# Norm factors spread over the partitions by way of DRAM, and the end of a convolution module written in a new order

## The chip, the cores and the metric

The kernel runs on one core of one Trainium2 chip. The metric is the device time of one execution in microseconds (us), and the smaller the better. A core has five engines that run side by side, each with its own list of instructions: TensorE (PE; its weight loads are shown as PEld), VectorE (DVE), ScalarE (ACT), GpSimd (POOL) and SyncE (SP). SP issues most of the DMAs, POOL those that add onto what stands in SBUF. An instruction starts when the one ahead of it on its engine is out of the way and the semaphores it waits for have been set.

## The reference

Four residual layers on 512 tokens of 1024 channels, all in float32: a mixer (retention and pooling), an FFN, a conformer convolution module, a second FFN. Every sub-layer reads its input through an RMS norm, and a last norm ends it. The parts that the change touches:

```python
def rms_norm(x, g):
    x32 = x.astype(jnp.float32)
    y = x32 * lax.rsqrt(jnp.mean(x32 * x32, axis=-1, keepdims=True) + EPS)
    return (y * g).astype(x.dtype)

def conformer_conv(h, w_pw1, b_pw1, w_dw, b_dw, ln_g, ln_b, w_pw2, b_pw2):
    a, gate = jnp.split(h @ w_pw1 + b_pw1, 2, axis=-1)
    u = a * jax.nn.sigmoid(gate)
    dw = lax.conv_general_dilated(
        u, w_dw[:, None, :], window_strides=(1,), padding=((CONV_WIDTH - 1, 0),),
        dimension_numbers=('NWC', 'WIO', 'NWC'), feature_group_count=D_MODEL) + b_dw
    d32 = dw.astype(jnp.float32)
    mu = jnp.mean(d32, axis=-1, keepdims=True)
    var = jnp.mean(jnp.square(d32 - mu), axis=-1, keepdims=True)
    z = (d32 - mu) * lax.rsqrt(var + EPS) * ln_g + ln_b
    z = jax.nn.silu(z).astype(h.dtype)
    return z @ w_pw2 + b_pw2

def swiglu(h, w_gate, w_up, w_down):
    return (jax.nn.silu(h @ w_gate) * (h @ w_up)) @ w_down
...
    for layer in range(DEPTH):
        ...
        h = h + swiglu(rms_norm(h, ffn_norm_g[layer]), ffn_w_gate[layer], ffn_w_up[layer], ffn_w_down[layer])
    return rms_norm(h, final_norm_g)
```

## The kernel before

**Tiling.** Activations lie with channels on the 128 partitions and the 512 tokens along the row, as eight tiles of 128 channels. Every large product is made of three: operand and weight are each split into a high part and a rest (`xgh`, `xgl`, `w`), and PE multiplies high by high, high weight by rest, rest weight by high (`mm3`, lines 199 to 201; each 128x512). `feature_major` runs over the eight k-tiles and two output tiles, 48 matmuls.

**The weights' split.** A chunk of weights (1 MB) comes by SP into `wr`. ACT copies it to the high part and writes its negative into the rest; then either DVE forms the rest (`split_load`, line 186), or a POOL DMA adds the raw chunk onto the negative (`split_load` lines 176 to 178, in the FFNs' chunk 2; `split_rest` lines 1351 to 1353, in the conv module). The latter are `w<-wr` on POOL in the profile. PE's third matmul (line 201) of a k-tile reads the rest, so it cannot start before that DMA has landed.

**The norms.** The norm's factor is one number a token. `token_sums` (line 281) sums the squares by matmuls whose weights are the 128 tokens of a block and whose moving operand is a column of ones; the result has tokens on the partitions, four columns (`ps_ms`). `rsqrt` makes the factors `rs_y` (128x4) on DVE by Newton steps. `spread` (lines 284 to 294) then brings them along the rows, the same on all partitions: four matmuls of a broadcast column with the identity into `ps_rms`, and an ACT copy to `bc_rms` (128x512). The factors are applied late, to the products: in the mixer to the rotations' cosine and sine (lines 497, 498), in the FFNs to `gu` in `hidden` (line 884), in the conv module to `gu` in `gated` (line 1191). This happens once in each of the four layers.

**The conv module.** `proj(j)` is the product for channel tile j (48 matmuls into `ps_pw`). `gated(j)` makes u: DVE scales by `bc_rms` (L1191), ACT takes the sigmoid (`act`, L1192), DVE joins them (L1196). The depthwise convolution of tiles 0 to 2 is done tap by tap on DVE (`some_taps`, L1329). For tiles 3 to 7, `to_rows` copies u by four DMAs into `R`, 32 partitions each (for tile 5 into the room of `zh`), and `conv_tile` (L1229) runs 32 matmuls of 32 columns, over 512 tokens, or over a half of 256 (A, then B) for tiles 6 and 7. `pivot_sum` takes sums of tiles 0 and 1 by PE, `pivot_tile` adds a tile to the running sums, `stats` has PE sum over the channels (L281), `spread` brings mean and scale along the rows (`mus`, `lrs`). Then `centre`, `swish`, `z_hi`, `z_lo` make the operand of the last product in pairs of tiles (`d`, `zh` L1288, `zl`), and `out_proj` runs the first two output pairs for half A, then for half B (`ps_p`, lines 220 to 223).

**What sets the order.** In the conv module the order on PE, DVE, ACT and SP is as the code is written (`manual_schedule`). In the other layers a scheduler places the instructions of each engine at build time; SP and POOL execute their lists in order as well. `split_rest` is a generator: `next(rest)` issues its first half, and `gated(..., rest)` the second half after the sigmoid. The PSUM tiles `aux` of `paux` (two) hold `ps_ms`, the spreads and the convolutions' results; `pair` gives tiles of two banks.

## Time and profile before

| what | us |
|---|---|
| median of three runs (1048.09 to 1048.49) | 1048.3 |
| the profiled execution, its own time | 1047.62 |
| its span, first instruction to last | 1045.8 |
| PE busy in the span | 1035.9 |
| DVE busy | 850.5 |
| ACT busy | 515.9 |
| POOL busy | 32.5 |

The granted TensorE clock was 0.998 over the span, so the clock plays no part. The layers on PE: the mixer to 182 us, the first FFN to 514, the conv module to 696, then the second FFN. "Idle before, releaser" behind a row is the time its engine stood still before it, and what it waited for. PE's starts lie closer together than its durations, since matmuls overlap: a 128x512 matmul takes 0.39 us in the records and the next one starts 0.23 us later.

### The profile page before, as it was taken

The numbers are of one execution on the slowest core, as the hardware profiler recorded it, in microseconds if no ns is written. First come the engines' busy times: TensorE is split into PE (matmuls) and PEld (weight loads), VectorE is DVE, ScalarE is ACT, GpSimd is POOL, SyncE is SP. The second block draws the span as 40 slices with busy tenths as digits, with TensorE's granted clock in tenths as the row PEclk, the third lists the DMA queues.
The fourth block names the chain that finished last, engine by engine and source line by source line (L and its number), as shares of the span: only waits on it lengthen the run. The fifth ranks groups of instructions, "written<-read, shape, count | busy, mean of one in ns | idle before, by whom it ended". The sixth has DMA issues, their size and how long they took to land.

```text
span 1045.8 us, 16517 instructions
## 1 busy us (share of the span) xinstructions
PE 1035.9 (99%) x6705; PEld 907.9 (87%) x6705; DVE 850.5 (81%) x1297; ACT 515.9 (49%) x881; POOL 32.5 (3%) x33
## 2 busy tenths in 40 slices
PE   9999999999999999999999999999999999999997
PEld 7878888899999999998888665988999999999987
DVE  7888735889988889997779797859999888899855
ACT  8543134765454545543444325656654455445434
POOL 0000000100000000001121100000000000000000
PEclk9999999999999999999999999999999999999999
DMA  8322122643323322333248996146233332323122
GB/s 300 132 81 81 41 81 88 184 136 116 111 92 104 119 91 92 122 118 125 81 94 188 222 189 149 59 139 174 72 121 121 102 121 76 112 96 122 41 81 81
DMA packets 38108, 121.63 MB, mean 116 GB/s; under 512 B 4112, under 2 KB 13328, under 8 KB 29584
## 3 DMA queue, kind: packets, MB, share of 16 engines
q1 hardware_dynamic: 34432, 107.99, 32.4%
q0 software_dynamic: 3456, 12.58, 6.3%
q8 instruction: 52, 0.85, 0.3%
q14 instruction: 24, 0.20, 0.1%
q10 hardware_dynamic: 144, 0.00, 0.0%
HBM read 100.36 MB, written 2.10 MB: 98 GB/s over the span
## 4 chain that ended last, share of the span: by engine, by line
PE 88%; DVE 6%; ACT 2%; DMA 2%; issue 1%; DVEq 0%; ACTq 0%
PE ps_x L854 19%; PE ps_y L854 10%; PE ps_dn L199 7%; PE ps_dn L200 7%; PE ps_dn L201 7%; PE ps_z L854 5%; PE ps_c L1229 2%; PE ps_gu L201 2%; PE ps_gu L199 2%; PE ps_gu L200 2%; PE ps_pw L199 2%; PE ps_pw L201 2%; PE ps_pw L200 2%; DMA wr<-in_w_pw 2%; PE ps_wo L201 1%; PE ps_wo L200 1%
## 5 line engine op out<-in xcount | busy, mean ns | idle before, releaser
L854 PE MATMUL ps_x<-th,w 128*128 128x256 f32 x608 | 115.9, 276 | 0.3 <-ACT sn L929 0.3
L765 DVE TENSOR_TENSOR wg<-wg 128x512 f32<-128x512 f32 x152 | 105.3, 693 | 5.1
L774 ACT CAST w<-wg 128x512 fp32r<-128x512 f32 x152 | 82.9, 618 | 37.3 <-PE ps_y L854 36.0
L854 PEld LDWEIGHTS ps_x<-th,w 128*128 128x128 f32 x608 | 97.2, 188 | 0.5 <-ACT sn L929 0.5
L779 DVE TENSOR_TENSOR w<-wg,w 128x2048 fp32r<-128x2048 f32 x38 | 87.1, 2291 | 10.5 <-ACT w L774 10.1
L854 PE MATMUL ps_x<-tl,w 128*128 128x256 f32 x304 | 83.9, 276 | 0.0
L311 DVE TENSOR_TENSOR X<-X,ps_dn 128x1024 f32<-128x1024 f32 x46 | 56.0, 1218 | 18.6 <-PE ps_dn L201 18.6
L183 ACT CAST w<-wr 128x2048 fp32r<-128x2048 f32 (+2 forms) x22 | 34.8, 1599 | 56.6 <-PE ps_g L573 21.8
L199 PE MATMUL ps_dn<-hh,dh0d 128*128 128x512 f32 x152 | 59.4, 391 | 0.0
L200 PE MATMUL ps_dn<-hl,dh0d 128*128 128x512 f32 x152 | 59.4, 391 | 0.0
L201 PE MATMUL ps_dn<-hh,dl0d 128*128 128x512 f32 x152 | 59.2, 390 | 0.1
L854 PE MATMUL ps_y<-th,w 128*128 128x256 f32 x304 | 57.9, 276 | 0.0
L854 PE MATMUL ps_y<-xgh,w 128*128 128x256 f32 x304 | 57.9, 276 | 0.0
L854 PEld LDWEIGHTS ps_x<-tl,w 128*128 128x128 f32 x304 | 57.1, 188 | 0.0
L939 ACT COPY sn<-ps_x 128x256 f32<-128x256 f32 x38 | 14.2, 374 | 85.9 <-PE ps_x L854 85.9
L200 PE MATMUL ps_dn<-hl,dh1d 128*128 128x512 f32 x144 | 56.2, 391 | 0.0
L199 PE MATMUL ps_dn<-hh,dh1d 128*128 128x512 f32 x144 | 56.2, 391 | 0.0
L201 PE MATMUL ps_dn<-hh,dl1d 128*128 128x512 f32 x144 | 56.0, 389 | 0.0
L854 PE MATMUL ps_x<-xgh,w 128*128 128x256 f32 x288 | 55.2, 277 | 0.0
L878 DVE TENSOR_TENSOR hl<-act,hh 128x512 fp32r<-128x512 f32 x44 | 30.5, 692 | 26.3 <-ACT hh L877 26.1
L877 ACT CAST hh<-act 128x512 fp32r<-128x512 f32 x44 | 27.3, 621 | 48.0 <-DVE act L872 44.0
L199 PE MATMUL ps_pw<-xgh,w 128*128 128x512 f32 x128 | 50.3, 393 | 0.0
(346 smaller groups left out, 3098.9 us busy)
## 6 DMA issues: line engine op xcount, KB each, us to landing
wg<-in_w_gu SPq DMA_DIRECT2D x38, 1024.0 KB, 4.9
dr<-in_w_dn SPq DMA_DIRECT2D x64, 256.0 KB, 2.9
w<-wr POOLq DMA_DIRECT2D x24, 512.0 KB, 5.3
wr<-in_w_pw SPq DMA_DIRECT2D x10, 1024.0 KB, 5.1
wr<-in_w_gu SPq DMA_DIRECT2D x6, 1024.0 KB, 4.9
dr<-in_w_dn SPq DMA_DIRECT2D x32, 192.0 KB, 2.5
wr<-in_w_o SPq DMA_DIRECT2D x4, 1024.0 KB, 4.9
R<-u SPq DMA_DIRECT2D x12, 270.0 KB, 14.6
```

What stands on the lines that cost most here:

```text
L183: nc.scalar.copy(wh[:, s], raw[:, s])
L199: nc.tensor.matmul(out, lhsT=wh, rhs=xh, start=start, stop=False)
L200: nc.tensor.matmul(out, lhsT=wh, rhs=xl, start=False, stop=False)
L201: nc.tensor.matmul(out, lhsT=wl, rhs=xh, start=False, stop=stop)
L311: nc.vector.tensor_tensor(xx, xx, ps, sign)
L765: nc.vector.tensor_tensor(o, o, i, ALU.add)
L774: nc.scalar.copy(block(sums[f][0], *SUMS[i]), block(raw_g[f], *SUMS[i]))
L779: nc.vector.tensor_tensor(l, raw_g[f], h.bitcast(F32), ALU.subtract)
L854: nc.tensor.matmul(out, lhsT=u[:, k, :], rhs=v, start=first and k == 0 and n == 0, stop=k == 3 and n == 2, skip_group_check=True)
L877: nc.scalar.copy(hh[f], s)
L878: return lambda: nc.vector.tensor_tensor(hl[f], s, hh[f].bitcast(F32), ALU.subtract)
L1229: nc.tensor.matmul(ps[32 * i:32 * i + 32, :n], lhsT=dgs[j][:, i, g, :], rhs=Rs[j][:, i, 4 * g + cols.start:4 * g + cols.stop], start=g == ...
```

## The change

There are two parts.

First, the four spreads of the norms' factors (`rms`) no longer use PE and ACT. A new `spread_row` has SP write `rs_y` (128x4, 2 KB) into a row in DRAM (`row_rms`) and then read that row back with the same 512 numbers to all 128 partitions (`bc_rms`, 256 KB). For the row to be in the order of the tokens, `token_sums(by=NT)` now takes as weights every fourth token (a partition then holds four neighbouring tokens) in both FFNs and the conv module; the mixer keeps its blocks and writes the row with four-byte pieces. The spreads of the conv module's `mu` and `lrs` stay on PE.

Second, the conv module from tile 5's gate on is written anew:

- The sigmoids of `gated(5)` and `gated(6)` stand ahead of the ACT copies of the weights' split, which come after the rows' DMAs.
- `pivot_sum` comes after 18 taps instead of 14; the spread of the pivot stands before group 4 of tile 4's convolution instead of 5.
- Tile 5's convolution runs in two halves, as those of 6 and 7; the gate of tile 7 too. PE's order is c5 A, c6 A, c5 B (first half), c7 A, c5 B (second half), statistics of A, c6 B, c7 B.
- `out_proj` does the products with the high parts for all four output tiles first, then those with the rests `zl`; the spread of B's mean stands in its midst.
- The first pair of half B is scaled and activated tile by tile.

```diff
+    dr = ctx.enter_context(tc.tile_pool(name="dr", bufs=2, space=bass.MemoryType.DRAM))
...
-    def token_sums(acc, cols=FULL):
+    def token_sums(acc, cols=FULL, by=1):
...
+        if by > 1:
+            for t in range(n):
+                nc.tensor.matmul(ps[:, t:t + 1], lhsT=acc.rearrange("p (q t) -> p t q", t=n)[:, t, :], rhs=ones,
+                                 start=True, stop=True)
+            return ps[:, :n]
...
+    def spread_row(v, name, tokens="(p t) -> p t"):
+        row = dr.tile([S], F32, tag="row", name=f"row_{name}")
+        out = wk.tile([P, S], F32, tag=f"bc_{name}", name=f"bc_{name}", bufs=1)
+        nc.sync.dma_start(row.rearrange(tokens, t=NT), v)
+        nc.sync.dma_start(out, row.partition_broadcast(P))
+        return out
...
-            rb = spread(rtok, "rms")
+            rb = spread_row(rtok, "rms", "(t p) -> p t")
...
-        r = inv_rms(acc)
+        row["rb"] = spread_row(inv_rms(acc), "rms")
...
-        feature_major(ps[1], *w, xgh, xgl, between={5: lambda: row.update(rb=spread(r, "rms"))})
+        feature_major(ps[1], *w, xgh, xgl)
...
-                proj(1, {2: lambda: note("rb", spread, row["r"], "rms")})
-                rb = row["rb"]
+                rb = spread_row(row["r"], "rms")
+                proj(1)
...
-                rest = split_rest()
-                next(rest)
                 c3 = conv_tile(3, FULL)
                 some_taps(1)
-                gated(5, pss[5], FULL, two_taps, rest)
+                gated(5, pss[5], FULL, two_taps)
                 start_load()
                 to_rows(5, FULL)
+                for _ in split_rest():
+                    pass
                 bias_tile(3, c3)
-                some_taps(14)
+                some_taps(18)
...
-                some_taps(8)
-                into_sums(2)
-                c5 = conv_tile(5, FULL)
-                gated(7, pss[7], FULL)
-                to_rows(7, A)
-                start_load()
-                to_rows(7, B)
+                into_sums(2, two_taps)
+                some_taps(NDVE * CW)
+                pivot_tile(4, c4, FULL)
+                into_sums(1)
+                p5 = pair("ps_c5")
+                c5 = conv_tile(5, A, ps=p5[:, 0, :])
+                for cols in HALVES:
+                    gated(7, pss[7], cols)
+                    to_rows(7, cols)
+                    if cols is A:
+                        start_load()
...
                 c6 = conv_tile(6, A, ps=p6[:, 0, :])
-                pivot_tile(5, c5, FULL)
+                pivot_tile(5, c5, A)
+                c5 = conv_tile(5, B, ps=p5[:, 1, :], groups=range(4))
                 c7 = conv_tile(7, A, ps=p7[:, 0, :])
...
+                conv_tile(5, B, ps=p5[:, 1, :], groups=range(4, 8))
...
-                swish(0, B)
-                z_hi(0, B)
+                for i in range(2):
+                    di = d[:, i, B]
+                    nc.vector.tensor_tensor(di, di, lrs[:, B], ALU.mult)
+                    nc.scalar.activation(di, di, AF.Silu, scale=V("ln_g", i), bias=V("ln_b", i))
+                    nc.scalar.copy(zh[:, i, B], di)
```

Where the instructions stand, as the built programs have them (no time is in this). Line numbers of after.py run one or two above those of before. **PE at the end of the conv module.** Tile 5 reads its rows from `zh`, tile 6 from `R_5673` (before) or `R_5663` (after), tile 7 from `R_5834` or `R_5837`; x32 is 32 matmuls. Before:

```order
L1229 MATMUL ps_c_5794<-zh,zf_5033 32x512 x32
L1229 MATMUL ps_c_5856<-R_5673,zf_5034 32x256 x32
L1229 MATMUL ps_c_5857<-R_5834,zf_5034 32x256 x32
L1229 MATMUL ps_c_5856<-R_5673,zf_5034 32x256 x12
L281 MATMUL ps_ms<-con,acc 128x1 x2
L281 MATMUL ps_ms<-con,s_5039 128x1 x2
L1229 MATMUL ps_c_5856<-R_5673,zf_5034 32x256 x16
L289 MATMUL ps_mu<-con,mean 128x128 x2
```

And after:

```order
L1231 MATMUL ps_c_5797<-zh,zf_5029 32x256 x32
L1231 MATMUL ps_c_5854<-R_5663,zf_5030 32x256 x32
L1231 MATMUL ps_c_5797<-zh,zf_5029 32x256 x16
L1231 MATMUL ps_c_5855<-R_5837,zf_5030 32x256 x32
L1231 MATMUL ps_c_5797<-zh,zf_5029 32x256 x16
L274 MATMUL ps_ms<-con,acc 128x1 x2
L274 MATMUL ps_ms<-con,s_5035 128x1 x2
L1231 MATMUL ps_c_5854<-R_5663,zf_5030 32x256 x16
```

Half of tile 5's convolution now lies behind tile 6's first half and around tile 7's, and the twelve matmuls of c6 B that stood ahead of the statistics stand behind them.

**ACT in the conv module,** from the sigmoid of tile 4 (`act`) to that of tile 6. Before:

```order
L1192 ACTIVATE act<-gu,vec 128x512
L1351 CAST w_5444<-wr_5351 128x1024
L1352 ACTIVATE w_5444<-w_5444 128x1024
L1351 CAST w_5527<-wr_5433 128x1024
L1352 ACTIVATE w_5527<-w_5527 128x1024
L1192 ACTIVATE act<-gu,vec 128x512
L1351 CAST w_5527<-wr_5433 128x1024
L1352 ACTIVATE w_5527<-w_5527 128x1024
L1242 ACTIVATE d<-ps_c_5531,vec 128x512
```

And after:

```order
L1194 ACTIVATE act<-gu,vec 128x512
L1353 CAST w_5437<-wr_5344 128x1024
L1354 ACTIVATE w_5437<-w_5437 128x1024
L1194 ACTIVATE act<-gu,vec 128x512
L1353 CAST w_5570<-wr_5426 128x1024
L1354 ACTIVATE w_5570<-w_5570 128x1024
L1353 CAST w_5570<-wr_5426 128x1024
L1354 ACTIVATE w_5570<-w_5570 128x1024
L1244 ACTIVATE d<-ps_c_5520,vec 128x512
```

The sigmoid of tile 5 no longer stands behind the copy that waits for the chunk `wr_5433`.

**SP in the conv module.** The row and its broadcast stand between the last chunk loaded ahead and the next one. After:

```order
L148 DMA wr_5052<-in_w_pw 128x2048
L294 DMA row_rms<-rs_y 128x4
L295 DMA bc_rms<-row_rms 128x512
L148 DMA wr_5184<-in_w_pw 128x2048
L148 DMA wr_5268<-in_w_pw 128x2048
```

Before, the same chunk loads followed one another with nothing between them; in the other three layers the two DMAs are put in likewise, and POOL's list is unchanged.

**PE in the mixer.** Here the scheduler has moved some matmuls. `ps_p` with `yh` is the pooling's group map, `ps_v` a projection. The third group's rows before:

```order
L571 MATMUL ps_v_800<-w_657,xgh_107 128x512
L572 MATMUL ps_v_800<-w_657,xgh_107 128x512
L199 MATMUL ps_p_726<-yh,pwh 128x512
L573 MATMUL ps_v_800<-w_657,xgl_108 128x512
L571 MATMUL ps_v_800<-w_657,xgh_109 128x512
```

And after:

```order
L573 MATMUL ps_v_799<-w_656,xgh_109 128x512
L574 MATMUL ps_v_799<-w_656,xgh_109 128x512
L575 MATMUL ps_v_799<-w_656,xgl_110 128x512
L200 MATMUL ps_p_725<-yh,pwh 128x512
L573 MATMUL ps_v_799<-w_656,xgh_111 128x512
```

The matmul that reads `yh` stands one matmul of `ps_v` later than before; the second group's likewise, the first group's stands where it stood, the fourth's some ten rows later.

More of the change, by code (lines that the diff above doesn't have):

```diff
@@ L294, in spread @@
         return out
+    def spread_row(v, name, tokens="(p t) -> p t"):
[4 more added lines that the diff above has]
+        return out
     def inv_rms(acc):
         v = sm.tile([P, NT], F32, tag="ms", name="ms")
[L298 removed]
+        nc.vector.tensor_scalar(v, token_sums(acc, by=NT), 0.5 / D, 0.5 * EPS, ALU.mult, ALU.add)
         return rsqrt(v, NT, "a4")
@@ L1430, in conv @@
                 pivot_mean()
-                gated(6, pss[6], FULL, two_taps, rest)
+                gated(6, pss[6], FULL, two_taps)
                 to_rows(6, FULL)
-                c4 = conv_tile(4, FULL, {5: lambda: spread(row["piv"], "mu", piv)})
-                some_taps(4)
+                for _ in split_rest():
+                    pass
+                c4 = conv_tile(4, FULL, {4: lambda: spread(row["piv"], "mu", piv)})
+                some_taps(6)
                 nc.vector.scalar_tensor_tensor(s1, piv, -2.0, dsum, ALU.mult, ALU.add)
@@ L1463, in conv @@
                 centre(2, A)
-                rest = pivot_tile(6, c6, B, True)
                 swish(2, A)
@@ L1467, in conv @@
                 z_lo(0, A)
-                rest()
+                pivot_tile(6, c6, B)
                 centre(4, A)
@@ L1472, in conv @@
                 z_lo(2, A)
-                rest = pivot_tile(7, c7, B, True)
+                later = pivot_tile(7, c7, B, True)
                 centre(6, A)
-                rest()
+                later()
                 swish(6, A)
@@ L1484, in conv @@
                 note("B", stats, B)
-                out_proj(w1, 4, A)
-                spread(row["B"][0], "mu", mus[:, B])
+                out_proj(w1, 4, A, lambda: spread(row["B"][0], "mu", mus[:, B]))
                 spread(row["B"][1], "lrs", lrs[:, B])
```

48 lines of the change are left out of this document (22 added, 26 removed).

## The prediction

> **What bounds the kernel now.** I read the page's busy times and its chain first, then the waits of PE alone, then the timeline of each engine at the places that the change touches.
>
> ```profile
> PE 1035.9 (99%) x6705; PEld 907.9 (87%) x6705; DVE 850.5 (81%) x1297; ACT 515.9 (49%) x881; POOL 32.5 (3%) x33
> ...
> PE 88%; DVE 6%; ACT 2%; DMA 2%; issue 1%; DVEq 0%; ACTq 0%
> ```
>
> PE is busy for 1035.9 of the span's 1045.8 us. Little is to be had from its waits; time falls if PE has less to do, and only if what PE comes to next is ready earlier too. What the matmuls waited for, but for the first instruction of all (total, times, longest):
>
> ```profile
> PE ps_p L222 <- ACT zh L1288: 0.8, 2, 0.5
> PE ps_ms L281 <- DVE acc L1301: 0.3, 1, 0.3
> PE ps_x L854 <- ACT sn L929: 0.3, 1, 0.3
> PE ps_ms L281 <- DVE acc L256: 0.2, 1, 0.2
> ```
>
> The conv module owns the first two (1.1 us), and the change rewrites both places.
>
> **What the removed spreads cost.** Four times eight short matmuls and one ACT copy go:
>
> ```profile
> L289 PE MATMUL ps_rms<-con,rs_y x32: 271/275/275, 31.3 to 715.5; 128*128 128x128 f32 x32
> L293 ACT COPY bc_rms<-ps_rms x4: 566/568/588, 32.4 to 718.1; 128x512 f32<-128x512 f32 x4
> ```
>
> In the first FFN PE's list reads (start, duration):
>
> ```profile
> 200.47 0.39 PE L201 MATMUL ps_gu<-xgh,w 128*128 128x512 f32 x1
> 200.70 1.05 PE L289 MATMUL ps_rms<-con,rs_y 128*128 128x128 f32 x8
> 201.51 0.48 PE L199 MATMUL ps_gu<-xgh,w 128*128 128x512 f32 x1
> 201.82 0.39 PE L200 MATMUL ps_gu<-xgl,w 128*128 128x512 f32 x1
> ```
>
> Without the eight, the matmuls of 201.51 and 201.82 would start 0.23 and 0.46 after 200.47: 200.70 and 200.93. So a spread is worth 201.82 - 200.93 = 0.9 us of PE, four of them 3.6. The sum now asks, for each, what PE meets next.
>
> **Mixer: 0.2 of 0.9.**
>
> ```profile
> 40.47 0.69 DVE L497 TENSOR_TENSOR cosr<-cosr,bc_rms 128x512 f32<-128x512 f32 x1 [3.88 <-ACT cosr L494]
> ```
>
> ```profile
> 64.67 0.39 PE L200 MATMUL ps_u<-xgl,w 128*128 128x512 f32 x1
> 65.15 0.50 PE L199 MATMUL ps_p<-yh,pwh 128*128 128x512 f32 x1
> ...
> 81.06 0.39 PE L572 MATMUL ps_v<-w,xgh 128*128 128x512 f32 x1
> 81.51 0.50 PE L199 MATMUL ps_p<-yh,pwh 128*128 128x512 f32 x1
> ```
>
> The factors' first reader, DVE at 40.47, waits for ACT's cosine, not for the spread at 31, so the trip by DRAM lies in 9 us of cover. But the chain from that cosine through the rotations to `yh` runs on DVE and ACT and does not move. At 65.15 PE is already 0.25 late (0.48 after its neighbour instead of 0.23) because it waits for `yh`; coming there 0.9 sooner it waits 1.15. The spread gives nothing there. At 81.51 another 0.22 is lost to `yh`; there the new order puts one matmul of `ps_v` ahead, 0.23, which covers it. I take 0.2; bounds 0 and 0.9.
>
> **Both FFNs: 0 of 1.8.** This is where I expect the expected gain to go. The weight loads just behind the spread:
>
> ```profile
> 206.16 0.19 PEld L201 LDWEIGHTS ps_gu<-xgh,w 128*128 128x128 f32 x1 [0.26 <-DMA w<-wr]
> ```
>
> ```profile
> 720.29 0.19 PEld L201 LDWEIGHTS ps_gu<-xgh,w 128*128 128x128 f32 x1 [0.41 <-DMA w<-wr]
> ```
>
> These are the first matmuls of `ps_gu` that read the rest of chunk 2. PE already waits there for the POOL DMA that makes that rest. What sets its landing is not PE at 200:
>
> ```profile
> 199.10 1.05 ACT L176 CAST w<-wr 128x1024 fp32r<-128x1024 f32 x1 [0.26 <-DMA wr<-in_w_gu]
> 200.18 1.06 ACT L177 ACTIVATE w<-w 128x1024 fp32r<-128x1024 f32 x1
> ```
>
> ```profile
> 201.53 0.86 POOL L178 DMA_DIRECT2D w<-wr  x1 [11.78 <-ACT w L177]
> ```
>
> The chunk's load ends, ACT copies and negates, POOL issues: a chain that the change does not touch. PE gets there 0.9 sooner and waits 0.9 longer, in both FFNs. The ACT copy that goes stands behind those two and shortens nothing. The DRAM trip has cover here, from the last step of `rs_y` to its first reader:
>
> ```profile
> 197.99 0.16 DVE L271 SCALAR_TENSOR_TENSOR rs_y<-rs_t,rs_y 128x4 f32<-128x4 f32 x1
> ...
> 206.75 1.22 DVE L884 TENSOR_TENSOR gu<-ps_gu,bc_rms 128x1024 f32<-128x1024 f32 x1
> ```
>
> These are 8.6 us. Bounds for the two: +1.0 if the 256 KB of the broadcast hold up each POOL DMA by half a microsecond, -1.8 if the landing moves along. I take 0.
>
> **Conv module: the trip.** Here the factors are wanted at once:
>
> ```profile
> 532.45 0.16 DVE L271 SCALAR_TENSOR_TENSOR rs_y<-rs_t,rs_y 128x4 f32<-128x4 f32 x1
> ...
> 536.44 1.23 DVE L1191 TENSOR_TENSOR gu<-ps_pw,bc_rms 128x1024 f32<-128x1024 f32 x1 [3.79 <-ACT bc_rms L293]
> ```
>
> From `rs_y` to the gate were 3.8 us by PE and ACT. Neither new DMA is in the trace; the nearest rows, and the largest for a plain load:
>
> ```profile
> dr<-in_w_dn SPq DMA_DIRECT2D x64, 256.0 KB, 2.9
> wr<-in_w_pw SPq DMA_DIRECT2D x10, 1024.0 KB, 5.1
> dr<-in_w_dn SPq DMA_DIRECT2D x32, 192.0 KB, 2.5
> ```
>
> Two legs, one behind the other: at least 2.5 + 2.9 = 5.4, at most 2 x 5.1 = 10.2. I take 5.4, with two POOL DMAs in flight beside it: DVE starts its gates about 1.6 late, 6.4 at the upper end. Only the gate stands behind the trip, since SP's next transfer was at 541:
>
> ```profile
> 541.61 24.68 SPq L147 DMA_DIRECT2D wr<-in_w_pw  x3
> ```
>
> Does PE feel the delay? DVE is full from 536 to the sums:
>
> ```profile
> 587.09 1.23 DVE L1191 TENSOR_TENSOR gu<-ps_pw,bc_rms 128x1024 f32<-128x1024 f32 x1 [0.67 <-PE ps_pw L201]
> 588.23 0.74 DVE L1329 SCALAR_TENSOR_TENSOR d<-zf,vec,d 128x512 f32<-128x512 f32 x1
> 588.89 0.75 DVE L1329 SCALAR_TENSOR_TENSOR d<-u,vec,d 128x512 f32<-128x512 f32 x1
> 594.76 0.75 DVE L1196 SCALAR_TENSOR_TENSOR u<-gu,vec,act 128x512 f32<-128x512 f32 x1 [5.12 <-ACT act L1192]
> ```
>
> ```profile
> 605.45 1.05 PE L281 MATMUL ps_ms<-con,acc 128*128 128x1 f32 x8 [0.29 <-DVE acc L1301]
> ```
>
> With the sigmoid ahead of the splits the 5.1 us of idle DVE before 594.76 go; four more taps at 0.66 (588.89 - 588.23) cost 2.7. With the 0.7 idle at 587.09 also at hand, the sums for 605.45 are ready at 605.4 - 0.7 - 5.1 + 2.7 = 602.3 plus the delay d. PE, 0.9 sooner and without the wait, wants them at 604.3. For d below 2.0 the spread's 0.9 is kept here and the 0.3 goes as well.
>
> **Conv module: the end.** Tile 5 in halves costs no PE time: the convolution runs at 7 us for a tile and 3.5 for a half.
>
> ```profile
> 625.76 7.07 PE L1229 MATMUL ps_c<-zh,zf 128*32 128x512 f32 x64
> 632.66 8.38 PE L1229 MATMUL ps_c<-R,zf 128*32 128x256 f32 x152
> ```
>
> But c6 A now stands behind half of c5, so it comes at 625.76 - 1.2 + 3.5 = 628.0 instead of 632.7, and needs the rows of tile 6:
>
> ```profile
> 610.87 4.35 SPq L1207 DMA_DIRECT2D R<-u  x4
> ```
>
> ```profile
> R<-u SPq DMA_DIRECT2D x4, 270.0 KB, 15.3
> ```
>
> The fourth is issued at about 614.5 and lands 15 us later, near 629: a **new wait** of up to 1.1. u6 is made sooner, but its DMAs stand on SP behind a chunk's load and tile 5's rows in queues that are full; I take 0.6, bounds 0 and 1.1. Behind it, the two waits for `zh` (0.8) are what the earlier statistics and the tile-by-tile gate of half B aim at: PE reaches `out_proj` A with the pair ready. For half B, statistics and `zh` follow a chain of DVE and ACT that I find 0.3 short of PE (bounds 0 and 0.7). The rests `zl` are off the path: sixteen matmuls with the high parts now run ahead of the first that reads them.
>
> Sum for the module: 0.9 + 0.3 + 0.8 - 0.6 - 0.3 = 1.1.
>
> **The strided weights.** `token_sums` takes every fourth float of a row as weights. The trace has no such load; beside it are
>
> ```profile
> L281 PEld LDWEIGHTS ps_ms<-con,acc x48: 186/192/192, 24.2 to 707.6; 128*128 128x128 f32 x48
> ```
>
> I take no cost, since the eight loads are the whole of a passage of about 1 us (605.45) and in the FFNs lie ahead of the wait for the landing anyway; bound: twice the passage, 1.0 more in the conv module alone. The Trainium skill, Advanced Engine Details and Errata, section Memory Cachelines, says that SBUF is read in lines of 16 bytes and that an access that meets a new line each time pays a penalty: a step of four floats is just that. No run here shows it; by that rule the sum would be about nothing instead of 1.3, and I keep it as a rival.
>
> **Sum.** 0.2 + 0 + 1.1 = 1.3 us. From the profiled execution's 1047.62 that is 1046.3; the median of the three runs lies 0.7 above it, so **1047.0**.
>
> **Rivals.**
> - *All four spreads are kept*: the landings in the FFNs and `yh` in the mixer move with PE. 3.6 + 0.2 from the conv end: 1044.5. Against it stand the two DMA waits above. Chance 0.10.
> - *No new waits at the conv end*: tile 6's rows come in time, half B too. 0.2 + 0.9 + 0.3 + 0.8 = 2.2, and restarts of PE behind waits that go, up to 0.4: 1045.7 to 1046.1. For it speaks the sooner u6. Chance 0.20.
> - *The strided loads take twice as long*, eight of them exposed in the conv module: 1.3 - 1.0 = 0.3, 1048.0. Chance 0.12.
> - *Slower: the trip by DRAM is late in the conv module.* PE passes the sums at 602.3 + d instead of 605.45, so from d = 3.2 (a trip of 7.0 us) the module is behind where it was. At d = 6.4 it is 3.2 late; the conv end gives back 0.8 (the wait for tile 6's rows is then covered), the mixer 0.2, and a broadcast that slow also holds up the POOL DMAs of the FFNs, up to the 1.0 of their bound: +3.2, 1051.5. Half of that delay beyond 3.2 and half of that bound give +1.1, 1049.4. For it: two POOL DMAs of 512 KB run beside the trip. Against it: the loads of 256 KB above. Chance 0.13.
>
> **How the numbers follow.** The forecast itself has 0.45, with 1046.0 to 1047.9 as its own range by the bounds of its terms. A measurement of this kernel tells about 0.2%, 2.1 us, from no change; faster means below 1046.2. Faster: the first rival, most of the second, a tail of the forecast: 0.10 + 0.16 + 0.07 = 0.33. Slower, above 1050.4: 0.09, the worse part of the last and what I have not seen. Between: 0.58. The range, 1045.1 to 1049.5, leaves out the first rival and the upper part of the last.
>
> **What would show it.** Right: PE rows without `ps_rms`; the weight loads of chunk 2 in both FFNs idle about 1.1 and 1.3 for `w<-wr` instead of 0.26 and 0.41, starting at unchanged distance from the layer's start; the wait at `ps_p` <- `yh` grown to about 1; the gate of tile 0 some 5.4 after `rs_y`; no wait for `acc` at the pivot; a wait of PE before c6 A. Wrong: no DMA wait in the FFNs; the weight loads of `ps_ms` above 0.19 in the conv module; the gate of tile 0 over 7 us behind `rs_y`, with PE waiting before c3 or the pivot.

## The result, and the profile after

| | median, us | range of the runs | ratio to before, 95% interval |
|---|---|---|---|
| before, same chip | 1048.19 | 1047.44 to 1048.49 | |
| after | 1060.9 | 1058.07 to 1063.97 | 1.0123 [1.0094, 1.0152] |

The change makes the kernel slower by 12.7 us, where 1047.0 with a range up to 1049.5 had been forecast. The profiled execution of after took 1063.97 us, the longest of its four, so its rows add up to 16.3 us and not to 12.7. Three executions in the runs further below took 1.4 to 2.6 times as long as all the others (1491.09, 2213.01 and 2703.92 us), and no ratio counts them.

The page of after, busy times and chain:

```profile
PE 1042.9 (98%) x6737; PEld 914.2 (86%) x6737; DVE 850.3 (80%) x1303; ACT 514.5 (48%) x880; POOL 32.6 (3%) x33
...
PE 84%; DMA 7%; DVE 4%; ACT 3%; issue 1%; POOL 0%; DVEq 0%; SPq 0%; ACTq 0%; POOLq 0%
```

The span grew by 16.4 (1045.8 to 1062.2). DMA now holds 7% of the chain where it had 2%. PE lost four times eight short matmuls (the count is higher by 32 all the same, since tile 5's convolution in halves has 64 more), and yet it is busy for 7.0 us more: a part of its matmuls ran at a lower clock, as is seen below.

What PE waited for in after (total, times, longest):

```profile
PE ps_u L200 <- DVE qk L513: 5.4, 1, 5.4
PE ps_c L1231 <- DMA R<-u: 3.7, 1, 3.7
PE ps_pw L202 <- DMA w<-wr: 0.9, 1, 0.9
...
PE ps_gu L202 <- DMA w<-wr: 0.6, 1, 0.6
```

The two waits of before that the change aimed at (0.8 for `zh`, 0.3 at the pivot) are gone. In their place stand one in the mixer and two in the conv module that before did not have.

Where the distance grows is told by the first and last starts of a tile's matmuls, before and then after. Of each kernel these are groups of the tiles `ps_wo` (the mixer's last product), `ps_x` (the FFNs), `ps_pw` (the conv module's projections), `ps_p` (its last product), with count, duration min/median/max, and first and last start:

```profile
L199 PE MATMUL ps_wo<-mh,w x64: 387/389/482, 136.7 to 181.4; 128*128 128x512 f32 x64
L854 PE MATMUL ps_x<-th,w x608: 276/276/386, 219.4 to 996.8; 128*128 128x256 f32 x152
L199 PE MATMUL ps_pw<-xgh,w x128: 389/389/499, 514.2 to 625.0; 128*128 128x512 f32 x128
L222 PE MATMUL ps_p<-zh,w x64: 276/276/384, 649.6 to 673.6; 128*128 128x256 f32 x64
```

```profile
L200 PE MATMUL ps_wo<-mh,w x64: 386/390/482, 143.6 to 188.3; 128*128 128x512 f32 x64
L856 PE MATMUL ps_x<-th,w x608: 275/277/385, 226.4 to 1013.1; 128*128 128x256 f32 x152
L200 PE MATMUL ps_pw<-xgh,w x128: 388/390/629, 521.1 to 634.4; 128*128 128x512 f32 x128
L1378 PE MATMUL ps_p<-zh,w x64: 275/277/395, 665.3 to 688.9; 128*128 128x256 f32 x64
```

After is 6.9 us behind when the mixer ends, 7.0 and 6.9 at the two ends of the first FFN, 9.4 at the last projection, 15.7 at the last product of the conv module and 16.3 in the second FFN. So the mixer and the conv module are to be explained. The first FFN adds nothing and the second 0.6, the wait at `ps_gu` above.

**The mixer in after.** The list of SP, which issues the row and its broadcast (start, duration of the issue), and the line for the four rows and four broadcasts together:

```profile
30.20 0.38 SPq L294 DMA_DIRECT2D row_rms<-rs_y  x1
38.95 0.34 SPq L295 DMA_DIRECT2D bc_rms<-row_rms  x1
```

```profile
DMA to landing us min/median/max: 1.4/3.8/8.7
```

The broadcast waits for the row to land: 2 KB took 8.7 us. The broadcast took 5.6 more, so the factors were there near 44.6, where before had the cosine ready at 40.47. In this execution the cosine was later still, so DVE's last wait was for ACT and not for the broadcast:

```profile
45.47 0.69 DVE L499 TENSOR_TENSOR cosr<-cosr,bc_rms 128x512 f32<-128x512 f32 x1 [3.88 <-ACT cosr L496]
```

Why the cosine was late is seen in run 2. PE's list from 55 us on, and the granted clock by windows of 5 us (PE, PEld, DVE, ACT, POOL busy and their instructions, clock, DMA share, GB/s):

```profile
55.63 0.80 PE L200 MATMUL ps_u<-xgh,w 128*128 128x512 f32 x1 [5.45 <-DVE qk L513]
56.22 0.63 PE L201 MATMUL ps_u<-xgl,w 128*128 128x512 f32 x1
56.65 0.63 PE L202 MATMUL ps_u<-xgh,w 128*128 128x512 f32 x1
```

```profile
50.00:55.00 5.00, 0.19 (x1) 0.00 (x0) 5.00 (x7) 2.21 (x4) 0.00 (x0) 0.89 0.40 118
55.00:60.00 5.00, 4.37 (x10) 3.51 (x11) 4.57 (x6) 4.22 (x5) 0.00 (x0) 0.50 0.24 97
```

PE stands still for 5.4 us until DVE has turned the last `qk`, and then runs at half its clock: a matmul starts every 0.43 us, not every 0.23. The twelve starts from 55.63 to 60.84, where the clock is back, take 5.2 us instead of 2.7. These 2.5 and the wait of 5.4, less the spread's 0.9 that is gone, are about the mixer's 6.9.

### The profile page after: what moved, and what is told of

The parts are those of the page before. It is cut to its first block, busy times and chain, and to the rows that moved or that the text cites. A ratio compares the mean times of both kernels' runs of the same rounds, so it can differ in the third digit from the quotient of the medians.

```text
span 1062.2 us, 16591 instructions
## 1 busy us (share of the span) xinstructions
PE 1042.9 (98%) x6737; PEld 914.2 (86%) x6737; DVE 850.3 (80%) x1303; ACT 514.5 (48%) x880; POOL 32.6 (3%) x33
## 4 chain that ended last, share of the span: by engine, by line
PE 84%; DMA 7%; DVE 4%; ACT 3%; issue 1%; POOL 0%; DVEq 0%; SPq 0%; ACTq 0%; POOLq 0%
PE ps_x L856 19%; PE ps_y L856 10%; PE ps_dn L201 7%; PE ps_dn L200 7%; PE ps_dn L202 6%; PE ps_z L856 5%; DMA wr<-in_w_pw 2%; DMA w<-wr 2%; PE ps_c L1231 2%; DMA R<-u 2%; PE ps_gu L202 1%; PE ps_wo L200 1%; PE ps_wo L201 1%; PE ps_wo L202 1%; PE ps_gu L200 1%; PE ps_gu L201 1%
## 5 line engine op out<-in xcount | busy, mean ns | idle before, releaser
L781 DVE TENSOR_TENSOR w<-wg,w 128x2048 fp32r<-128x2048 f32 x38 | 87.0, 2290 | 10.7 <-ACT w L776 10.5
L202 PE MATMUL ps_pw<-xgh,w 128*128 128x512 f32 x128 | 50.8, 397 | 0.9 <-DMA w<-wr 0.9
L200 PE MATMUL ps_pw<-xgh,w 128*128 128x512 f32 x128 | 51.0, 398 | 0.0
## 6 DMA issues: line engine op xcount, KB each, us to landing
R<-u SPq DMA_DIRECT2D x12, 270.0 KB, 15.3
```

The lines of the kernel that those rows point to most:

```text
L200: nc.tensor.matmul(out, lhsT=wh, rhs=xh, start=start, stop=False)
L202: nc.tensor.matmul(out, lhsT=wl, rhs=xh, start=False, stop=stop)
L781: nc.vector.tensor_tensor(l, raw_g[f], h.bitcast(F32), ALU.subtract)
```

## The experiments

Each kernel was timed against before on the same chip, and the ratio is given with its 95% interval; in the fourth digit it can differ from the quotient of the two medians beside it. The first four runs take the mixer and the FFNs apart from the conv module.

**1. The mixer's trip alone.**

```diff
-            rb = spread(rtok, "rms")
+            rb = spread_row(rtok, "rms", "(t p) -> p t")
```

> The kernel before with the mixer's spread alone taken by DRAM, as in the change (a row of 512 pieces of four bytes, then the broadcast); all else on PE. Theory A (the mixer's row of four-byte pieces holds up the load of the pooling weights, ACT's copy of them stands ahead of the cosine, PE waits for the rotations and then runs at half clock for a while): slower by 6 to 8 us, 1054 to 1056, with the pooling weights landing near 39, the cosine's factor applied near 45.5, a PE wait of about 5.4 and a granted clock near 0.5 behind it. Rival B (the loss of the first 145 us comes from the whole of the change, as shared DMA or a clock that differs from run to run): within 2 us of before.

Measured: 1053.99 against 1047.99, ratio 1.0053 [1.0038, 1.0068], that is +6.0 us. Its profile shows the trip on DVE without any other cause beside it: the pooling's weights, which the expectation blamed, were with ACT at 33.18. It also shows the time to landing of the broadcast (6.1) and the row (8.1):

```profile
44.77 0.69 DVE L512 TENSOR_TENSOR cosr<-cosr,bc_rms 128x512 f32<-128x512 f32 x1 [7.83 <-DMA bc_rms<-row_rms]
```

```profile
DMA to landing us min/median/max: 6.1/7.1/8.1
```

The factors arrive 14.3 us after the row was issued at 30.43. The cover ended at 40.47. About half of the whole loss is here.

**2. Does the slow row hurt by its lateness, or by what it holds up?** The 512 pieces are written as in run 1, but nobody reads the row; the factors come by PE as before.

```diff
+            aside = dr.tile([S], F32, tag="row", name="row_rms")
+            nc.sync.dma_start(aside.rearrange("(t p) -> p t", t=NT), rtok)
```

> The kernel before, with PE's spread kept in the mixer, and beside it the same write of the factors into DRAM in 512 pieces of four bytes, which nothing reads. Theory A1 (the write itself holds up the pooling weights, and ACT's order does the rest): pooling weights land near 39 instead of 31.5, ACT's copy of them near 38.8, and the loss is nearly the whole of the mixer's, 5 to 8 us. Rival A2 (the loss is the late broadcast, 44.6, which the cosine's factor must wait for; the pooling weights only happened to be late): pooling weights near 31.5 to 33, time within 1 us of before.

Measured: 1048.04 against 1047.99, ratio 1.0002 [0.9993, 1.0012]. By the median the write alone costs nothing, so run 1's loss is the wait for the broadcast. One thing remains: in the profiled execution of this run, the longest of its ten (1050.16), PE waited 2.4 us for `qk` all the same. There, as in after's profile, a neighbour was late, the pooling's weights, and ACT's copy of them stands ahead of the cosine. In after:

```profile
38.80 0.62 ACT L219 CAST pwh<-pw 128x512 fp32r<-128x512 f32 x1 [8.42 <-DMA pw<-in_pool_w]
```

These weights (256 KB, issued some 4 us ahead of the row) took 5.5 us to land in before, 6.9 in run 1, 10.7 in run 2 and 13.0 in after; in none of the profiles without a row in the mixer did ACT wait for them. So the write of many small pieces also holds up a transfer beside it, by an amount that changes from one execution to the next. In after's profile this set the time of the cosine; the broadcast alone would have done so some 0.8 sooner.

**3. The same trip with the row written in 128 pieces of 16 bytes.**

```diff
-            rb = spread(rtok, "rms")
+            rb = spread_row(rtok, "rms", "(p t) -> p t")
```

> The mixer's spread by DRAM with the row written in 128 pieces of 16 bytes, as the FFNs and the conv module write theirs; the order of the tokens in the row is then another, so the rotations' factors are those of other tokens. Theory A (the four-byte pieces are the cause): row lands within 2 us, the broadcast about 4 us later, near 36; pooling weights near 32; no PE wait for the rotations; 0 to 0.5 us faster than before, as my forecast had it for the mixer (0.2). Rival C (any trip by DRAM at this place costs, since it competes with the loads of the weights): slower by 2 us or more.

Measured: 1048.17 against 1047.99, ratio 1.0002 [0.9993, 1.0012]. The row now takes 1.9 us, the broadcast 3.5, and `cosr` waits again for the cosine alone:

```profile
DMA to landing us min/median/max: 1.9/2.7/3.5
```

```profile
40.38 0.69 DVE L512 TENSOR_TENSOR cosr<-cosr,bc_rms 128x512 f32<-128x512 f32 x1 [3.88 <-ACT cosr L509]
```

The piece size is thus the mixer's whole loss: 16 bytes for four make the row's 8.1 us into 1.9, and the broadcast's 6.1 into 3.5. And the 0.9 of the spread does not come out as time: PE waits 0.7 for `yh` and 0.6 for `qk` and neither stands in before's list of waits; the forecast argued so of `yh`.

**4. Both FFNs' trips alone,** with the strided sums.

```diff
-        r = inv_rms(acc)
+        row["rb"] = spread_row(inv_rms(acc, NT), "rms")
...
-        feature_major(ps[1], *w, xgh, xgl, between={5: lambda: row.update(rb=spread(r, "rms"))})
+        feature_major(ps[1], *w, xgh, xgl)
```

> The kernel before with the two FFNs' spreads alone by DRAM (with every fourth token as weights in the sums). My forecast's step: PE's freed time is taken by the wait for the rest of chunk 2, so the time is within 1 us of before, with the weight loads that wait for it in both FFNs, and no wait elsewhere; in the trace of the change the sums' eight strided loads take 0.85 us longer, so 0.9 freed less 0.85 leaves 0 in the first FFN, and in the second the landing is some 0.6 late: 0 to +1 us. Rival: the spreads' 1.8 us are gained.

Measured: 1048.17 against 1047.99, ratio 0.9998 [0.9988, 1.0008]. Nothing is won and nothing lost.

**5. The conv module's new order alone,** all spreads on PE as before. Against after, in the mixer and the conv module (the FFNs' spreads go back likewise, and the sums are of contiguous blocks again):

```diff
-            rb = spread_row(rtok, "rms", "(t p) -> p t")
+            rb = spread(rtok, "rms")
...
-                rb = spread_row(row["r"], "rms")
-                proj(1)
+                proj(1, {2: lambda: note("rb", spread, row["r"], "rms")})
+                rb = row["rb"]
```

> The change's new order of the conv module alone: all four spreads of the norms are on PE and ACT as before. Theory D (the trip by DRAM makes the first gate of the conv module 2.7 us late, that lateness runs down ACT's splits, POOL's DMAs, the weight loads and SP to the rows of tile 6, and c6 A, which now stands 3.5 us earlier, waits for them): here no trip, so the rows are in time within about 1 us, and the time is -1.5 to +1 us against before. Rival E (the new order by itself makes the rows late, since ACT's split now stands behind the gates and SP's row transfers): +4 to +7 us already here, with a wait of PE for the rows before c6 A of 3 us or more.

Measured: 1048.57 against 1047.42, ratio 1.0014 [1.0003, 1.0024], +1.2 us, a little above the first theory's range. The waits for `zh` and at the pivot are gone, and one has come:

```profile
635.65 3.66 PE L1231 MATMUL ps_c<-R,zf 128*32 128x256 f32 x64 [1.00 <-DMA R<-u]
```

It stands behind the first half of c5 B, so it is c7 A that waits, for the rows of tile 7. Tile 6's rows came in time here.

**6. The conv module's trip alone,** in the old order.

```diff
-                proj(0, {7: lambda: note("r", inv_rms, acc)})
+                proj(0, {7: lambda: note("r", inv_rms, acc, NT)})
...
-                proj(1, {2: lambda: note("rb", spread, row["r"], "rms")})
-                rb = row["rb"]
+                rb = spread_row(row["r"], "rms")
+                proj(1)
```

> The kernel before, with the conv module's spread alone by DRAM, sums by every fourth token, and the module's old order. Theory D: the first gate is about 5.4 after the factors, 1.6 to 2.7 later than before, but c6 A still stands behind the whole of c5, with 3.6 us of room for its rows; there is a wait of up to 1 for a rest of the weights, 0.85 for the strided loads, against 0.9 freed: 0 to +3 us. Rival E: about 0, all the loss is in the new order. A third, F (the trip alone loses it all): +5 to +7.

Measured: 1051.22 against 1047.42, ratio 1.0036 [1.0024, 1.0047], +3.8 us, between what the theories gave. A second run of the same kernel gave the profile that is read below:

> The same kernel as the run with the trip in the conv module and the old order (+3.8 us), for a profile. Theory D: the sums' eight loads at 0.33 us and a granted clock under 1 for about 3 us behind them; the first gate 2 to 3 us late against the layer's start; PE waits of 1 to 2 us for the rests; no wait for tile 6's rows, or less than 1.

Measured: 1051.54 (one time). DVE's first gate waits for the broadcast, and PE then waits for rests of the weights' split, which before it never did in this module:

```profile
539.84 1.23 DVE L1206 TENSOR_TENSOR gu<-ps_pw,bc_rms 128x1024 f32<-128x1024 f32 x1 [5.53 <-DMA bc_rms<-row_rms]
```

```profile
PE ps_pw L202 <- DMA w<-wr: 2.9, 2, 1.5
```

**7. Trip and new order together,** the other spreads on PE, and **8. the same with the sums taken by contiguous blocks** of 128 tokens, as before, in place of every fourth float.

```diff
-        nc.vector.tensor_scalar(v, token_sums(acc, by=NT), 0.5 / D, 0.5 * EPS, ALU.mult, ALU.add)
+        nc.vector.tensor_scalar(v, token_sums(acc), 0.5 / D, 0.5 * EPS, ALU.mult, ALU.add)
```

> The conv module as the change has it, trip and new order, the other three spreads on PE. All theories: the change's 12.7 less the mixer's 6.0 and the FFNs' 0.2 is 6.5, so +5 to +8 us. Theory D: clearly more than the two parts alone added up; E: as much as the new order alone; F: as much as the trip alone.

> The same as the run with trip and new order, but the sums take blocks of 128 tokens as weights, as before, so the factors reach other tokens. It prices the strided loads: 0.85 us of PE in the conv module, and the low clock of 3 us that followed them in the change's profiled execution. If the low clock comes from the eight slow loads behind a short wait, this run is 2 us or more faster than the one with strided loads, and the rows of tile 6 come 1 to 2 us earlier in the layer; if not, about 0.9 faster or less.

Measured: 1053.26 against 1047.42, ratio 1.0059 [1.0041, 1.0077], and 1051.28, ratio 1.0035 [1.0022, 1.0048]. So the conv module loses 5.8 us, about the other half of the whole. The order alone and the trip alone make 5.0 together, so "clearly more than the two parts" is not shown. Of the 5.8, 2.0 are the strided weights: the two intervals overlap, but all four times of run 7 (from 1052.35) lie above all five of run 8 (to 1051.78). The loads themselves, in the profile of after (`L269` strided, `L274` contiguous), and the clock around them, in run 7 and then in run 8:

```profile
L274 PEld LDWEIGHTS ps_ms<-con,acc x24: 187/192/193, 24.4 to 671.4; 128*128 128x128 f32 x24
...
L269 PEld LDWEIGHTS ps_ms<-con,acc x24: 308/330/332, 199.7 to 724.1; 128*128 128x128 f32 x24
```

```profile
525.00:535.00 10.00, 9.75 (x37) 7.88 (x36) 5.26 (x18) 3.66 (x6) 1.28 (x1) 0.83 0.01 0
```

```profile
525.00:535.00 10.00, 9.78 (x47) 7.95 (x46) 5.18 (x18) 5.72 (x8) 2.09 (x2) 1.00 0.01 0
```

A strided load takes 0.33 us for 0.19, and in run 7 the window of the eight loads holds 37 matmuls, not 47, at a granted clock of 0.83. The Trainium skill, Advanced Engine Details and Errata, section Memory Cachelines, has the rule that an SBUF access pays when each one meets a new 16-byte line; the loads agree with it. The eight loads hold PE for 1.90 us in run 7 and for 0.91 in run 8, so they are 1.0 of the 2.0; the rest is the lower clock. That drop does not belong to the strided loads alone: in the profile of run 6, with the same loads, this window was at 1.00 with 43 matmuls, and in that of run 13 below, with contiguous loads behind a wait of 1.0 us, it came:

```profile
530.00:540.00 10.00, 8.97 (x36) 6.86 (x35) 4.80 (x17) 5.59 (x7) 0.65 (x1) 0.83 0.01 1
```

**9. Are the late splits the rest?** The ACT copies of the second half of a split stand behind the sigmoid of a gate for tiles 1 to 4 (`rest` in `gated`). A gate that is 1.5 us late (537.91 in run 8, 536.44 in before) makes the sigmoid late, and with it the copy, the POOL DMA and PE's third matmul. Run 9 is run 8 with both halves of the split ahead of the sigmoid, in four places like this one.

```diff
                 rest = split_rest()
-                next(rest)
+                for _ in rest:
+                    pass
```

> As the run with trip, new order and blocks (+3.7 us, 3.3 of it in two waits of PE for a rest of the weights in tiles 4 and 5 of the projection), except that for tiles 2 to 5 both halves of the split stand ahead of the gate's sigmoid on ACT. If the late gate runs down ACT into the splits (theory D), the second halves are issued about 2 to 5 us sooner, the waits for the rests fall under 1 us in all, and the time is within 1.5 us of the kernel before. Rival H (the waits for the rests come from crowded queues, whatever ACT does): the waits and the time stay within 1 us of those of the other run.

Measured: 1047.72 against 1047.59, ratio 0.9999 [0.9990, 1.0008]. From 1.0035 to 0.9999 are 3.8 us. ACT's list in run 8 and in run 9, from the first half of a split on:

```profile
542.48 1.06 ACT L1353 CAST w<-wr 128x1024 fp32r<-128x1024 f32 x1 [2.59 <-PE ps_pw L202]
...
549.53 0.72 ACT L1194 ACTIVATE act<-gu,vec 128x512 f32<-128x512 f32 x1 [4.90 <-DVE gu L1193]
550.16 1.03 ACT L1353 CAST w<-wr 128x1024 fp32r<-128x1024 f32 x1
```

```profile
542.49 1.06 ACT L1353 CAST w<-wr 128x1024 fp32r<-128x1024 f32 x1 [2.63 <-PE ps_pw L202]
...
544.54 1.04 ACT L1353 CAST w<-wr 128x1024 fp32r<-128x1024 f32 x1
...
549.50 0.73 ACT L1194 ACTIVATE act<-gu,vec 128x512 f32<-128x512 f32 x1 [2.82 <-DVE gu L1193]
```

The second copy comes 5.6 us earlier, the sigmoid at the same time as before it. PE's waits for `w<-wr` fall from 3.3 to nothing in the profile. The first gate is as late as in run 8 (537.88), and the broadcast is there as well, so neither the gate itself nor fuller DMA queues make the loss. Nor do the splits win time by standing first: without a trip they are worth nothing (run 12 against run 11, below). What a late trip costs here is the split that is queued behind its gate.

**The chain goes on to the rows.** SP's list in run 5 (no trip) and in run 7 (with trip): the load of the last chunk in quarters, then the rows of tile 5 and of tile 6.

```profile
592.60 13.67 SPq L145 DMA_DIRECT2D wr<-in_w_pw  x4
606.37 3.52 SPq L1209 DMA_DIRECT2D zh<-u  x4
610.07 3.58 SPq L1209 DMA_DIRECT2D R<-u  x4
```

```profile
597.01 13.86 SPq L145 DMA_DIRECT2D wr<-in_w_pw  x4
611.29 3.29 SPq L1209 DMA_DIRECT2D zh<-u  x4
614.69 3.55 SPq L1209 DMA_DIRECT2D R<-u  x4
```

A chunk is loaded where an earlier one has been split (SP waits there for the split's POOL DMA, 19.6 us in all in run 5 and 19.8 in run 7); with the splits late, the load is 4.4 late, and the rows behind it on SP 4.6. (In run 9, with the trip and the splits first, tile 6's rows are issued from 608.39, as early as without a trip.) PE is only 2.5 late (c5 A starts at 628.29 instead of 625.81), so c6 A waits, in run 7 and in after:

```profile
635.39 3.66 PE L1231 MATMUL ps_c<-R,zf 128*32 128x256 f32 x64 [3.44 <-DMA R<-u]
```

```profile
642.55 6.23 PE L1231 MATMUL ps_c<-R,zf 128*32 128x256 f32 x64 [3.69 <-DMA R<-u]
```

In after the same 64 matmuls also take 6.2 us instead of 3.7, with a granted clock of 0.60 and 0.72 in the two windows of 5 us from 640 on. The wait of 3.7 and these 2.6 are the 6.3 by which after falls back between the last projection and the last product. In run 8, where PE had already waited 3.3 for the rests of the splits, c6 A does not wait: the late splits are paid at one place or at the other.

**10 and 11. Where c5 B stands.** If the wait in run 5 comes from c6 A being moved ahead of c5 B, moving it back should undo it. Run 10 puts both halves of c5 B ahead of c6 A, run 11 the first half alone; both with all spreads on PE. (The expectation of run 10 takes the wait of run 5 for one for tile 6's rows; by its place it is for tile 7's.)

```diff
+                c5b = conv_tile(5, B, ps=p5[:, 1, :])
                 c6 = conv_tile(6, A, ps=p6[:, 0, :])
                 pivot_tile(5, c5, A)
-                c5 = conv_tile(5, B, ps=p5[:, 1, :], groups=range(4))
+                c5 = c5b
...
-                conv_tile(5, B, ps=p5[:, 1, :], groups=range(4, 8))
-                c6 = conv_tile(6, B, ps=p6[:, 1, :], between={0: lambda: note("A", stats, A), 4: lambda: spread(row["A"][0], "mu", mus[:, A])})
+                c6 = conv_tile(6, B, ps=p6[:, 1, :], between={4: lambda: note("A", stats, A)})
...
```

This is run 10; run 11 has only the part ahead of the dots, with `groups=range(4)`.

> The change's new order of the conv module with all spreads on PE, except that PE runs both halves of tile 5 ahead of c6 A (as before), with the statistics of half A in the middle of c6 B. With the order of the change the trace shows PE waiting 1.0 for tile 6's rows, which land at 635.5, 0.3 us of restart behind it, and the run was 1.2 to 1.5 us slower than before. Theory D: the moved c6 A is what costs; here the rows have 3.5 us more, no such wait, and the time is 0.5 to 1.5 us faster than before (my forecast's 0.3 and 0.8 without its 0.6). Rival G (the other parts of the new order, such as the late splits or the tile-by-tile gate, cost): still 0.5 us or more slower than before.

> The change's new order of the conv module with all spreads on PE, except that the first half of c5 B stands ahead of c6 A instead of behind it (its second half stays ahead of the statistics). Theory D (the order's loss is the 1.0 us wait for tile 6's rows, and the loss of the run with all of c5 first was the other wait, 1.3 for half A's operand, since the statistics came late): with 1.75 us more for the rows and the statistics where the change has them, both waits go, and the time is 1 to 1.5 us below that of the new order alone, so 0 to 0.7 us faster than before. Rival G: neither wait is the loss; 0.5 us or more slower than before.

Measured: 1048.35 against 1047.59, ratio 1.0003 [0.9994, 1.0012], and 1048.59 against 1048.11, ratio 1.0004 [0.9995, 1.0012]. The wait for the rows went in both; another as large came in its place, in run 10 and in run 11:

```profile
PE ps_p L1378 <- ACT zh L1290: 1.3, 1, 1.3
```

```profile
PE ps_c L1231 <- DVE acc L1260: 1.2, 1, 1.2
```

Three placements of half a convolution, and each leaves PE one wait of 1.0 to 1.3 us. Before has 1.1 in three. Runs 5, 10 and 11 cannot be told from each other by their intervals, and the gain over before that both expectations named did not come.

**12 and 13. Versions meant to win.** Run 12 keeps the spreads on PE, with the placement of run 11 and the splits first. Run 13 has the conv module's trip by DRAM with neither of its two costs: splits first, and contiguous weights, for which ACT writes the squares that the conv module's norm sums in an order in which the tokens of a block lie together.

```diff
+    def grouped(x):
+        return x.rearrange("p (t q) -> p q t", t=NT) if regroup["on"] else x
...
+    def in_fours(x):
+        return x.rearrange("p (q t) -> p q t", t=NT) if regroup["on"] else x
...
-            nc.scalar.activation(sq, X[:, k, :], AF.Square)
+            nc.scalar.activation(grouped(sq), in_fours(X[:, k, :]), AF.Square)
```

> The same, and for tiles 2 to 5 both halves of the weights' split stand ahead of the gate's sigmoid. The splits' rests and so the loads come a little sooner, with nothing lost: 0.3 to 1.3 us faster than before. If PE waits for the rests are no matter where PE does the spread, it is the same as the run before it.

> The conv module's trip by DRAM with what cost it taken away: ACT writes the squares in groups so that the sums' weights are contiguous (no strided load) and the factors are those of the right tokens, both halves of the split stand ahead of the sigmoid, and half of c5 B stands ahead of c6 A; the other three spreads on PE. Theory D: strided loads, the low clock behind them, the late splits and the moved c6 A were all of the conv module's loss, so now the spread's 0.9 us of PE is gained on top: 0.7 to 2 us faster than before. If the trip's late gate still reaches PE by another way, it is the same as before or slower.

Measured: 1048.37 against 1048.11, ratio 1.0003 [0.9994, 1.0011], and 1051.4, ratio 1.0023 [1.0013, 1.0033]. Run 12 is no faster than before, nor than run 11 (1048.59). Run 13 is 3.3 us slower, where a gain had been expected, and its profile (of the longest of its eleven executions, 1053.79) names one cause, the squares on ACT. In run 13 (six of the eight that are written in the new order, from 507 to 530 us) and in before, with durations min/median/max:

```profile
L251 ACT ACTIVATE sq<-X x6: 1119/1129/1152, 507.6 to 529.9; 128x512 f32<-128x512 f32 x6
```

```profile
L255 ACT ACTIVATE sq<-X x21: 614/617/621, 158.6 to 699.0; 128x512 f32<-128x512 f32 x21
```

A write in steps of 512 bytes makes a square slower on ACT, 1.13 us for 0.62. PE then waits three times for what stands behind the squares: 0.9 at the end of the first FFN (for `dl0d`, whose high part ACT casts), 0.6 at the first projection (for a split) and 1.0 at `ps_ms` for the sum of squares, against 0.2. The clock of 0.83 shown at run 8 follows the last of them. So run 13 replaced one cost by another, and does not tell whether a trip without either would win. No version measured beats before.

## Why the prediction was wrong

Its sum was 0.2 + 0 + 1.1 us won. Measured apart, the mixer loses 6.0, the FFNs 0.2, the conv module 5.8: 12.0 of the 12.7, the rest within the intervals.

- **Mixer, 0.2 won: the step that failed is "the trip by DRAM lies in 9 us of cover".** The trip takes 14.3, in run 1 as in after. It was never sized in that part; the size used later for the conv module (5.4 to 10.2, with an upper end already beyond the 9) came from loads of 192 KB and more, and the row in the mixer is of another kind: 512 pieces of four bytes. That the row goes out in four-byte pieces was plain from the code, and the sum passed over it: it lands after 8.1 to 9.0 us, one of 128 pieces after 1.4 to 1.9. The Trainium skill, DMA: Bandwidth & Descriptors, section Rules for kernel authors, says that a last dimension that is not contiguous becomes one descriptor for each element; the times agree with it, and this was the rule that spoke against the change. The rest of the step held: with a fast row (run 3) the spread is worth nothing here, since PE meets `yh`.
- **FFNs, 0 of 1.8: right** (run 4), and mostly for the reason given. PE's third matmul of chunk 2 does wait longer in after's second FFN, and hardly longer in the first:

```profile
213.14 0.19 PEld L202 LDWEIGHTS ps_gu<-xgh,w 128*128 128x128 f32 x1 [0.37 <-DMA w<-wr]
```

```profile
736.61 0.18 PEld L202 LDWEIGHTS ps_gu<-xgh,w 128*128 128x128 f32 x1 [1.06 <-DMA w<-wr]
```

  1.1 and 1.3 had been forecast. The difference is the strided loads, which use up most of the 0.9 before PE comes to that wait: the eight `ps_ms` of the first FFN hold PE for 1.66 us in after (199.91 to 201.57) and for 0.81 in before (192.95 to 193.76). The trip itself was in time.
- **The conv module's trip, 5.4 us: right in size.** DVE's first gate waits 5.3 to 5.5 for the broadcast. **The step that failed is "for d below 2.0 the spread's 0.9 is kept".** It followed the gate along DVE to the sums. It left out ACT, where the second half of each split stands behind the sigmoid, and thus POOL, PE's third matmul, SP's chunk load and the rows behind it. With the splits first (run 9) a delay of the same size costs nothing; with the splits behind, 3.8 us. The rival that had this trip late put its price at the sums too, and only from d = 3.2.
- **Strided weights, no cost: wrong.** A load takes 1.7 times as long, and the passage of eight twice as long, 1.0 us, as the bound and the rival had it. With the clock that fell behind it in run 7 the cost in the conv module is 2.0 us (run 7 against run 8), twice the bound: no term had the clock in it.
- **The conv module's end, +1.1 with all: wrong in sign.** A new wait before c6 A was forecast at 0.6, at most 1.1. With late splits it was 3.4 to 3.7, because tile 6's rows stand behind the chunk load on SP; the forecast knew the place, and took its time from before. (Its own rows give a bound of 1.8 there and not 1.1, since 614.5 and 15.3 make 629.8.) Without the trip there is no such wait, but one of 1.0 at c7 A. So the order alone costs 1.2 [0.3, 2.5] where it should have given 0.2.
- **The range** was too narrow for two reasons: the cost of an operation that the trace did not show (the four-byte row) had been bounded by rows of another kind, and the late gate had been followed down one engine only. Of the 12.7 us the two failed steps are 6.0 in the mixer and 3.8 in the conv module (run 8 against run 9); the strided weights are 2.0 more.

What stays open: whether the new order really costs 1 us or is the same as before (run 5's interval just leaves out no change, those of runs 10 to 12, with half a convolution moved, take it in); what decides whether the clock falls behind a short wait; and what a trip with contiguous weights in the order of the tokens would give if they came without the cost on ACT.

## What to carry to other kernels

Replacing a few short matmuls by a trip through DRAM pays only if the trip's pieces are long (here 16 bytes, not four) and if what stands behind the reader has slack on every engine, not on the reader's alone: look at what each in-order queue holds behind the instruction that now waits. A layout that makes a later step simple (every fourth float) is paid for at each read, so its cost belongs in the sum, as a load of 0.33 us for 0.19. And an engine's idle time that was removed by writing an order anew tends to come back at the next thing that is late; count the waits of the new order before counting the old ones as won.

## What the runs showed of the hardware that was not expected

- A row of 2 KB written as 512 pieces of four bytes needs 8.1 to 9.0 us until it has landed, as 128 pieces of 16 bytes 1.4 to 1.9.
- The same write held up a load of 256 KB issued some 4 us ahead of it: landed after 6.9, 10.7 and 13.0 us in the three profiles that have it, after 5.3 and 5.5 in run 3 and in before.
- Behind waits of 3.7, 4.6 and 5.4 us (after, run 1, after) PE was granted half its clock for 3 to 5 us, which cost 1.6 to 2.6 us more; behind waits of 2.4 and 3.4 us (runs 2 and 7) it was not. But the clock also fell behind waits of 0.2 to 0.3 us with eight strided loads (run 7 and after; in run 6, with the same loads, it did not) and behind one of 1.0 us with eight contiguous loads (run 13).
- ACT writes a square of 128x512 floats in steps of 512 bytes in 1.13 us, and in order in 0.62.
